# Decoder trunk: the second half of the output projection computed as the first half is, two column chunks at a time with seven products for two of its row pairs

## The chip, the cores and the metric

The kernel runs on one core of a Trainium2 chip. The metric is the device time of one execution in microseconds (us). One execution was recorded by the hardware profiler; all rows shown are from that one.

## The reference

Two layers work on x (256 tokens x 2048, float32). Each layer computes

```
h   = RMSNorm(x)
P   = h @ W_in                 2048 x 6144: [q | k | v | gate_B | gate_C | conv_in]
A   = differential attention (8 heads, relative bias)
Cv  = gate_B * causal_conv3(gate_C * conv_in)
x   = x + concat([A, Cv]) @ W_out             2048 x 2048
x   = x + (relu(RMSNorm(x) @ W_up) ** 2) @ W_down     2048 x 8192, 8192 x 2048
```

The change touches `x + concat([A, Cv]) @ W_out` alone, and the moment at which the norm after it is prepared.

## The kernel before

Every float32 operand is split into a high and a low part in the format that TensorE multiplies (ACT copies the high part, DVE subtracts it from the value), and each product is made of three matmuls, high x high, high x low, low x high (`TERMS`). A matmul has 128 rows of the contraction, 128 tokens and 512 columns. Tokens come in two blocks of 128 (`t`), x in four column chunks of 512 (`xs[0]` to `xs[3]`).

*The output projection.* The contraction over 2048 rows goes in eight pairs of 128-row blocks. Chunks 0 and 1 are computed side by side by `BySeven.project` (L824), chunks 2 and 3 one after the other by `linear` (L390 to L409, called at L986). `project` holds two accumulators of two PSUM banks each, one for each chunk. Six row pairs are ordinary: 24 matmuls for two chunks (`plain`, L830). The other two (pairs 4 and 5, the first two of the convolution's four) are computed as a 2 x 2 block product with seven products in place of eight (`seven`, L852): sums of the blocks of activations are made beforehand (`sums_of`), sums of the blocks of weights in the jobs of L778, and four of the seven products go to banks of their own (three from the pool `ps`, tag `bank`, one with tag `av`); the other three go straight into the accumulators. After the last seven, `e1` to `e4` are made from these four banks by ACT and DVE (L892 to L896) and added to x (L895 and L902).

*The order.* `self.order` (L756 to L760) lists the steps: pairs 0 and 1 for chunk 0, then for chunk 1; seven, pair, seven, pair; then the last two pairs for chunk 0 and for chunk 1. When chunk 0 is complete (`done`), its accumulators and the e-terms are added to x. PE runs its instructions in the order in which the program records them; a scheduler orders ACT, DVE and the DMA queues.

*Weights.* `Weights.take` (L374) makes the splits of weights three steps ahead (`AHEAD`). Each plain step loads 512 KB into one of four `raw` buffers, by SP's queue, and a load waits until the split of the load four before it has read its buffer. The split halves stand in three buffers each (`hi`, `lo`). A seven takes two raw buffers at once and keeps them until its sums are made; it makes three splits of 1024 columns and one of 512.

*The norm after it.* `Norm.chunk` (L465) prepares one chunk of x for the up projection: squares on ACT, then eight 128x128 transposes on PE into two banks of the pool `ps` (tag `bank`, three banks in all, shared with the sevens' products), and four splits of 128x256 on each of ACT and DVE (`split_gained`, L287 and L288). `work.start(piece, wait)` puts it into a background list that counts ticks; a plain step has two ticks. At the end of `project`, chunk 0 is asked for after 2 ticks and chunk 1 after 4, both with 2 more of their own; chunks 2 and 3 are asked for when each is complete. After the last chunk, `Norm.factors` sums the squares (DVE), takes the power on POOL, and copies the result on DVE.

*The up projection* begins right behind (L1159). Its column 0 runs over rows of chunks 0 and 1 first, for two column blocks, then over chunks 2 and 3. Its weights come in 1 MB loads into four buffers; two of them lie where the projection's temporary tiles lay.

Of the kernel before, what the change touches and what calls it, by code (L numbers as in the profile page):

```python
# [9 lines left out]
F32 = mybir.dt.float32  # L10
# [5 lines left out]
P = 128  # L16
DEPTH = 2
D = 2048
S = 256
NT = S // P  # L20
# [8 lines left out]
CH = 512  # L29
# [93 lines left out]
def trunk(ctx: ExitStack, tc: tile.TileContext, x, w_in, w_out, conv_w, q_norm_g, k_norm_g,  # L123
# [19 lines left out]
    def bank(name):  # L143
        return ps.tile([P, CH], F32, tag="bank", name=name)
# [600 lines left out]
    class BySeven:  # L745
# [3 lines left out]
        def __init__(self, l, bpool, weights):  # L749
            self.l, self.pool, self.weights = l, bpool, weights  # L750
            n = D // (4 * P)
            seven = [n + q for q in GATED]
            plain = [i for i in range(2 * n) if i not in seven]


            self.order = [(n, i) for n in range(2) for i in plain[:2]]  # L756
            self.order += [step for i, j in zip(plain[2:], seven)
                           for step in (("seven", j), ("pair", i))]
            self.order += [("pair", i) for i in plain[2 + len(seven):-2]]
            self.order += [(n, i) for n in range(2) for i in plain[-2:]]  # L760
            self.sums = []

        def sums_of(self, q, y):
# [11 lines left out]
            nc.scalar.activation(hi, v, AF.Copy)  # L775
            nc.vector.tensor_sub(lo, v, hi.bitcast(F32))

        def jobs(self, w, i):  # L778

            mine = {}  # L780

            def split(hi, lo, src):
                nc.scalar.activation(hi, src, AF.Copy)
                nc.vector.tensor_sub(lo, src, hi.bitcast(F32))
                return hi, lo

            def two(pool, tag, name, src):

                room = pool.tile([P, 2, 2, CH], F32R, tag=tag, name=name)
                hi, lo = split(room[:, 0], room[:, 1], src)  # L790
                return [(hi[:, j], lo[:, j]) for j in range(2)]

            def plain():
                raws = []
                for n in range(2):
                    raw = self.weights.pool.tile([P, 2, CH], F32, tag="raw", name="raw", bufs=RAW)
                    nc.sync.dma_start(
                        raw, w[2 * P * i:2 * P * (i + 1), n * CH:(n + 1) * CH].rearrange(
                            "(k p) c -> p k c", p=P))
                    raws.append(raw)  # L800
                mine["raw"] = raws
                b11, b21 = two(self.pool, "b", "w7b", raws[0])
                hi = wpool.tile([P, 2, CH], F32R, tag="hi", name="whi")
                lo = wpool.tile([P, 2, CH], F32R, tag="lo", name="wlo")
                return b11, b21, split(hi[:, 0], lo[:, 0], raws[1][:, 1])

            def sums():
                left, right = mine["raw"]
                t = mine["t"] = self.pool.tile([P, 4, CH], F32, tag="b", name="w7t")

                nc.vector.tensor_sub(t[:, 0], right[:, 0], left[:, 0])
                nc.vector.tensor_sub(t[:, 1], right[:, 1], right[:, 0])
                made = two(apool, "a", "w7x", t[:, 0:2])

                nc.vector.tensor_add(t[:, 2], t[:, 1], left[:, 0])
                nc.vector.tensor_sub(t[:, 3], left[:, 1], t[:, 2])
                return made

            def more():
                return two(apool, "a", "w7y", mine["t"][:, 2:4])  # L820

            return [plain, sums, more]

        def project(self, cat, norm, kpool, tmp):  # L824
            weights = self.weights
            both = [mm.tile([P, NT, CH], F32, tag="mm2", name=f"o{self.l}{n}") for n in range(2)]
            accs = [[acc[:, t] for t in range(NT)] for acc in both]
            prods = {2: accs[0][0], 4: accs[0][1], 3: accs[1][0]}

            def plain(i, n):  # L830
                hi, lo = weights.take()
                for j in range(2):
                    k = 2 * i + j
                    a = cat[k // KG]
                    while not a.ready:
                        work.tick()
                    for t in range(NT):
                        for m, (pa, pw) in enumerate(TERMS):
                            nc.tensor.matmul(  # L839
                                accs[n][t], a.ap[:, pa, k % KG, t * P:(t + 1) * P],  # L840
                                (hi, lo)[pw][:, j], start=(k == 0 and m == 0),
                                stop=(i == last and j == 1 and m == 2))
                    work.tick()
# [8 lines left out]
            def seven(i, start, end):  # L852
                if start:
                    for n in (1, 5, 6):
                        prods[n] = bank(f"po{self.l}{n}")
                    prods[7] = ps.tile([P, CH], F32, tag="av", name=f"po{self.l}7", bufs=1)
                b11, b21, b22 = weights.take()
                t1, t3 = weights.take()
                t2, t4 = weights.take()
                for n, a, b in ((1, A11, b11), (2, A12, b21), (3, S4, b22), (5, S1, t1),  # L860
                                (7, S3, t3), (6, S2, t2), (4, A22, t4)):
                    own = n in (1, 5, 6, 7)
                    for m, (pa, pw) in enumerate(TERMS):
                        nc.tensor.matmul(prods[n], form(i, pa, a), b[pw],
                                         start=(start and own and m == 0),
                                         stop=(end and own and m == 2))
                    if n == 5:
                        work.tick()
                work.tick()

            def onto(n):
                for t in range(NT):
                    nc.vector.tensor_add(xs[n][:, t], accs[n][t], xs[n][:, t])

            last = self.order[-1][1]
            steps = [i for what, i in self.order if what == "seven"]
            done = [j for j, (what, i) in enumerate(self.order) if what == 0][-1]
            for j, (what, i) in enumerate(self.order):
                if what == "pair":
                    plain(i, 0)  # L880
                    plain(i, 1)
                elif what == "seven":
                    seven(i, i == steps[0], i == steps[-1])
                    if i == steps[-1]:

                        x11, x21, x12, x22 = (xs[n][:, t] for n in range(2) for t in range(NT))


                        room = tmp.tile([P, 2, CH], F32, tag="ao", name="es", bufs=1)
                        e1, e2, e3 = room[:, 0], wide("e2"), room[:, 1]  # L890
                        e4 = kpool.tile([P, CH], F32, tag="kL", name="es4")
                        nc.scalar.activation(e1, prods[1], AF.Copy)  # L892
                        nc.vector.tensor_add(e2, prods[6], e1)
                        nc.vector.tensor_add(e4, prods[5], e2)
                        nc.vector.tensor_add(x22, prods[5], x22)  # L895
                        nc.vector.tensor_add(e3, prods[7], e2)  # L896
                else:
                    plain(i, what)
                    if j == done:
                        onto(0)  # L900
                        for x_, e in ((x11, e1), (x12, e4), (x21, e3), (x22, e3)):
                            nc.vector.tensor_add(x_, x_, e)  # L902
            onto(1)
            for n in range(2):
                work.start(norm.chunk(n, 2), 2 * n + 2)


    def mixer(l, norm, loads):

        with ExitStack() as scope:  # L910
# [15 lines left out]
            for q in range(AW // WC):  # L926
                weights.turned(w_in[l], 3 * AW + q * WC)
            by_seven = BySeven(l, bpool, weights)
            for what, i in by_seven.order:
                if what == "seven":  # L930
                    weights.jobs += by_seven.jobs(w_out[l], i)
                    continue
                for n in ((0, 1) if what == "pair" else (what,)):
                    weights.plain(w_out[l], 2 * P * i, n * CH, 2)
            for n in range(2, D // CH):
                weights.straight(w_out[l], 0, D // P, n * CH)
            loads(weights)

            bias = biasp.tile([P, 2 * NH, S], F32, tag="bias", name="bias")
# [41 lines left out]
                    by_seven.sums_of(q, ys[:, q])  # L981

            mnorm = Norm(1, l)
            by_seven.project(cat, mnorm, kpool, tmp)
            for n in range(2, D // CH):
                acc = linear(f"o{l}{n}", cat, weights)  # L986
                for t in range(NT):
                    nc.vector.tensor_add(xs[n][:, t], acc[:, t], xs[n][:, t])
                work.start(mnorm.chunk(n, 2))
        return mnorm  # L990

    def mlp(l, mnorm, last):
# [479 lines left out]
```

## Time and profile before

| what | us |
|---|---|
| time, median of three runs (2124.51 to 2621.47) | 2124.92 |
| the profiled execution's own time | 2124.95 |
| its span, first to last instruction | 2123.2 |
| PE busy | 2117.0 |
| DVE busy | 1724.5 |
| ACT busy | 1377.2 |
| POOL busy | 159.2 |
| output projection of layer 0, chunks 0 and 1 (from, to) | 298.3, 340.5 |
| output projection of layer 0, chunks 2 and 3 (from, to) | 340.5, 386.9 |
| output projection of layer 1, first matmul | 1353.8 |

PE is TensorE, PEld its weight loads, which overlap with it, DVE VectorE, ACT ScalarE, POOL GpSimd, SP the queue that issues most DMAs. Matmuls are pipelined: one lasts 0.39 us, and the next starts 0.23 us after it. So busy time of PE does not count matmuls; their starts do. In rows of the timeline stand the start, the duration, engine, line, operation, what it writes and reads, and the count of merged instructions; in brackets the idle time before it and who ended it. In rows of groups stand busy time and the mean in ns of one.

### The profile page before, as it was taken

How to read it: one execution, taken by the hardware profiler on the slowest of the kernel's cores; microseconds unless marked ns; L12 is line 12 of the kernel's file. 1: busy time of each engine (PE TensorE's matmuls, PEld its weight loads, DVE VectorE, ACT ScalarE, POOL GpSimd, SP SyncE). 2: the span in 40 equal slices, each digit the busy share in tenths (PEclk: the TensorE clock that was granted, in tenths of full speed). 3: DMA queues.
4: the chain of work that ended last, by engine and by line, in shares of the span. 5: the costliest groups of instructions: out<-in, count | busy, mean ns of one | idle time of the engine just before them, and what ended most of it. 6: DMA issues, size and time to landing. Idle time of an engine off the chain costs nothing.

```text
span 2123.2 us, 29201 instructions
## 1 busy us (share of the span) xinstructions
PE 2117.0 (100%) x10857; PEld 1809.9 (85%) x10857; DVE 1724.5 (81%) x2388; ACT 1377.2 (65%) x1828; POOL 159.2 (7%) x226
## 2 busy tenths in 40 slices
PE   9999999999999999999999999999999999999999
PEld 7888888888888888888888888888888888888887
DVE  6777676798888888799766776767988888888997
ACT  6767555677777776666566765556677677675664
POOL 3010100000000000011101101000000000000110
PEclk9999999999999999999999999999999999999999
DMA  8556667677777777788656565666877777777993
GB/s 272 179 167 191 196 191 229 214 252 224 231 233 231 236 230 231 250 301 290 217 170 182 165 208 179 197 209 221 260 233 232 232 230 232 233 230 259 319 310 104
DMA packets 297743, 476.01 MB, mean 224 GB/s; under 512 B 12707, under 2 KB 193781, under 8 KB 297600
## 3 DMA queue, kind: packets, MB, share of 16 engines
q1 hardware_dynamic: 269120, 406.76, 60.7%
q0 software_dynamic: 28288, 67.24, 10.0%
q8 instruction: 85, 1.39, 0.3%
q14 instruction: 58, 0.48, 0.1%
q10 hardware_dynamic: 192, 0.15, 0.0%
HBM read 440.52 MB, written 33.58 MB: 223 GB/s over the span
## 4 chain that ended last, share of the span: by engine, by line
PE 99%; DMA 0%; DVE 0%; SPq 0%; ACT 0%; issue 0%; DVEq 0%
PE upc L1159 31%; PE pr L1202 14%; PE dn L1283 8%; PE ci L430 4%; PE gc L430 4%; PE gb L430 4%; PE k L405 4%; PE v L405 4%; PE o L405 4%; PE q L405 4%; PE o L839 3%; PE dn L1365 2%; PE dn L1202 2%; PE pr1r L1202 2%; PE pr0r L1202 1%; PE up L1159 1%
## 5 line engine op out<-in xcount | busy, mean ns | idle before, releaser
L320 DVE TENSOR_TENSOR wlo<-raw,whi 128x1024 fp32r<-128x1024 f32 x266 | 322.1, 1222 | 188.3 <-ACT whi L319 118.3
L1159 PE MATMUL upc<-nT,uhi 128*128 128x512 f32 x1920 | 454.7, 389 | 0.0
L319 ACT ACTIVATE whi<-raw 128x1024 fp32r<-128x1024 f32 x266 | 281.5, 1059 | 240.6 <-PE gb L430 28.2
L1159 PEld LDWEIGHTS upc<-nT,uhi 128*128 128x128 f32 x1920 | 360.3, 188 | 74.7
L1023 DVE TENSOR_TENSOR ulo<-uraw,uhi 128x1024 fp32r<-128x1024 f32 x256 | 311.8, 1221 | 119.3 <-ACT f L1191 89.4
L1022 ACT ACTIVATE uhi<-uraw 128x1024 fp32r<-128x1024 f32 x256 | 270.6, 1057 | 159.7 <-PE upc L1159 138.1
L1159 PEld LDWEIGHTS upc<-nT,ulo 128*128 128x128 f32 x1920 | 246.2, 191 | 9.4
L1159 PE MATMUL upc<-nT,ulo 128*128 128x256 f32 x1920 | 249.1, 283 | 0.0
L1283 PE MATMUL dn<-whi,fb 128*128 128x512 f32 x496 | 156.7, 389 | 0.0
L1048 ACT ACTIVATE b2h<-draw 128x1024 fp32r<-128x1024 f32 x83 | 88.2, 1062 | 48.5 <-PE pr L1202 41.3
L319 ACT ACTIVATE whi<-uraw 128x1024 fp32r<-128x1024 f32 x62 | 65.9, 1063 | 81.8 <-PE dn L1283 66.0
L1283 PEld LDWEIGHTS dn<-whi,fb 128*128 128x128 f32 x496 | 93.1, 188 | 19.3
L1169 ACT ACTIVATE ev<-upc 128x512 f32<-128x512 f32 x120 | 72.0, 600 | 54.0 <-PE upc L1159 54.0
L1048 ACT ACTIVATE t24h<-t 128x1024 fp32r<-128x1024 f32 x83 | 88.3, 1063 | 22.8 <-PE pr L1202 15.9
L1049 DVE TENSOR_TENSOR t24l<-t,t24h 128x1024 fp32r<-128x1024 f32 x83 | 101.1, 1218 | 1.7
L1049 DVE TENSOR_TENSOR b2l<-draw,b2h 128x1024 fp32r<-128x1024 f32 x83 | 100.9, 1215 | 1.1 <-ACT b2h L1048 1.1
L1049 DVE TENSOR_TENSOR t13l<-t,t13h 128x1024 fp32r<-128x1024 f32 x83 | 101.0, 1217 | 0.7
L1062 DVE TENSOR_TENSOR t<-draw 128x1024 f32<-128x1024 f32 x83 | 101.1, 1218 | 0.3
L1048 ACT ACTIVATE t13h<-t 128x1024 fp32r<-128x1024 f32 x83 | 88.4, 1065 | 13.3 <-DVE t L1062 2.9
L1283 PE MATMUL dn<-wlo,fb 128*128 128x512 f32 x248 | 96.5, 389 | 0.0
L1202 PE MATMUL pr<-t13h,f 128*128 128x512 f32 x240 | 93.8, 391 | 0.0
L320 DVE TENSOR_TENSOR wlo<-uraw,whi 128x1024 fp32r<-128x1024 f32 x62 | 75.7, 1222 | 18.0 <-ACT whi L319 17.6
(452 smaller groups left out, 4292.8 us busy)
## 6 DMA issues: line engine op xcount, KB each, us to landing
uraw<-in_w_up_dram SPq DMA_DIRECT2D x128, 1024.0 KB, 6.2
raw<-in_w_in_dram SPq DMA_DIRECT2D x191, 512.0 KB, 4.0
draw<-in_w_down_dram SPq DMA_DIRECT2D x174, 512.0 KB, 5.3
raw<-in_w_out_dram SPq DMA_DIRECT2D x64, 512.0 KB, 4.4
uraw<-in_w_down_dram SPq DMA_DIRECT2D x62, 512.0 KB, 5.7
raw<-in_w_down_dram SPq DMA_DIRECT2D x10, 1024.0 KB, 5.5
hid0p<-f POOLq DMA_DIRECT2D x19, 512.0 KB, 3.6
fb<-hid0p POOLq DMA_DIRECT2D x19, 512.0 KB, 6.8
```

The lines of the kernel that those rows point to most:

```text
L319: pair = (nc.scalar.activation(hi, raw, AF.Copy), nc.vector.tensor_sub(lo, raw, hi.bitcast(F32)))
L320: nc.vector.tensor_sub(lo, raw, hi.bitcast(F32)))
L405: nc.tensor.matmul(acc[:, t], a.ap[:, pa, k % KG, t * P:(t + 1) * P], (hi, lo)[pw][:, j], start=(k == 0 and (pa, pw) == (0, 0)), stop=(k = ...
L430: nc.tensor.matmul(acc[:, f, 0] if part else acc[:, f], wt[:, k % 4, fs], a.ap[:, 0, k % KG] if part else a.ap[:, :, k % KG], start=(part ...
L1022: pair = (nc.scalar.activation(hi, src, AF.Copy), nc.vector.tensor_sub(lo, src, hi.bitcast(F32)))
L1023: nc.vector.tensor_sub(lo, src, hi.bitcast(F32)))
L1048: keep(nc.scalar.activation(hi, src, AF.Copy))
L1049: keep(nc.vector.tensor_sub(lo, src, hi.bitcast(F32)))
L1062: keep(nc.vector.tensor_sub(t[:, 0:2], raw[:, :, 1], raw[:, 0]))
L1159: nc.tensor.matmul(acc[:, 0] if part else acc, wt[part][:, k], a.ap[:, 0, k % KG] if part else a.ap[:, :, k % KG], start=(part == 0 and kh ...
L1202: nc.tensor.matmul(prods[n], f[:, pa, a], b[pw], start=(start and m == 0), stop=(stop and m == 2))
L1283: nc.tensor.matmul(prods[p], f[:, pa, 2 * k + t], b[pw][:, n], start=(p in starts and k == 0 and m == 0), stop=(stop and k == 1 and m == 2))
```

## The change

`BySeven` keeps one order for each half of the columns. Half 0 has the order of before. Half 1 (chunks 2 and 3) has the same steps with each seven behind an ordinary pair. `project` is called for both halves and takes the half's number `g`; `linear` is not used for w_out any more. The chunks 0 and 1 of the norm are asked for after 2 and 6 ticks (2 and 4 before). Chunk 2 is asked for when it is complete, two plain steps before chunk 3 is, chunk 3 at the end as before. The additions of the e-terms to x have the order x11, x21, x12, x22 (x11, x12, x21, x22 before).

```
-            self.order = [(n, i) for n in range(2) for i in plain[:2]]
-            self.order += [step for i, j in zip(plain[2:], seven)
-                           for step in (("seven", j), ("pair", i))]
-            self.order += [("pair", i) for i in plain[2 + len(seven):-2]]
-            self.order += [(n, i) for n in range(2) for i in plain[-2:]]
+            self.orders = []
+            for g in range(2):
+                chunks = (2 * g, 2 * g + 1)
+                order = [(n, i) for n in chunks for i in plain[:2]]
+                for i, j in zip(plain[2:], seven):
+                    order += [("seven", j), ("pair", i)][::-1 if g else 1]
+                order += [("pair", i) for i in plain[2 + len(seven):-2]]
+                order += [(n, i) for n in chunks for i in plain[-2:]]
+                self.orders.append(order)
...
-        def jobs(self, w, i):
+        def jobs(self, w, i, col):
...
-                        raw, w[2 * P * i:2 * P * (i + 1), n * CH:(n + 1) * CH].rearrange(
+                        raw, w[2 * P * i:2 * P * (i + 1),
+                               col + n * CH:col + (n + 1) * CH].rearrange(
...
-        def project(self, cat, norm, kpool, tmp):
+        def project(self, g, cat, norm, kpool, tmp):
...
-                    plain(i, what)
+                    plain(i, what - 2 * g)
                     if j == done:
                         onto(0)
-                        for x_, e in ((x11, e1), (x12, e4), (x21, e3), (x22, e3)):
+                        for x_, e in ((x11, e1), (x21, e3), (x12, e4), (x22, e3)):
                             nc.vector.tensor_add(x_, x_, e)
+                        if g:
+                            work.start(norm.chunk(2 * g, 2), 2)
             onto(1)
+            if g:
+                work.start(norm.chunk(2 * g + 1, 2))
+                return
             for n in range(2):
-                work.start(norm.chunk(n, 2), 2 * n + 2)
+                work.start(norm.chunk(n, 2), 4 * n + 2)
...
-            for what, i in by_seven.order:
-                if what == "seven":
-                    weights.jobs += by_seven.jobs(w_out[l], i)
-                    continue
-                for n in ((0, 1) if what == "pair" else (what,)):
-                    weights.plain(w_out[l], 2 * P * i, n * CH, 2)
-            for n in range(2, D // CH):
-                weights.straight(w_out[l], 0, D // P, n * CH)
+            for g, order in enumerate(by_seven.orders):
+                for what, i in order:
+                    if what == "seven":
+                        weights.jobs += by_seven.jobs(w_out[l], i, 2 * g * CH)
+                        continue
+                    for n in ((2 * g, 2 * g + 1) if what == "pair" else (what,)):
+                        weights.plain(w_out[l], 2 * P * i, n * CH, 2)
...
-            by_seven.project(cat, mnorm, kpool, tmp)
-            for n in range(2, D // CH):
-                acc = linear(f"o{l}{n}", cat, weights)
-                for t in range(NT):
-                    nc.vector.tensor_add(xs[n][:, t], acc[:, t], xs[n][:, t])
-                work.start(mnorm.chunk(n, 2))
+            for g in range(2):
+                by_seven.project(g, cat, mnorm, kpool, tmp)
```

In the changed program the instructions of both layers stand in the same order on PE, ACT and DVE, and outside of the two output projections and the first column of the up projection the order on every engine is that of before. The order around the two places of which the prediction speaks, with what an instruction waits for:

```
PE: 2 steps of chunk 2; 8 transposes of x[0]; 2 steps of chunk 3; 4 transposes of x[1];
    4 transposes of x[1]  [wait: DVE's split of k = 1 of x[0], the last reader of the first bank]
ACT: squares of x[1]; whi; w7b [wait: its raw load]; whi; nT_0 k0, k2; whi; nT_0 k1, k3; ...
DVE: wlo; wlo; w7b; wlo; nT_0 k0; w7t, w7t; nT_0 k2; wlo; nT_0 k1; w7t; nT_0 k3; ...

PE: last product of chunk 3; 8 transposes of x[2]; 8 matmuls up; 4 transposes of x[3];
    4 transposes of x[3]  [wait: DVE's split of k = 1 of x[2]]; 8 matmuls up; ...
ACT: uhi; nT_2 k0; squares x[3]; nT_2 k2; squares x[3]; uhi; nT_2 k1; ...
DVE: x[3] +=; x[3] +=; ulo; nT_2 k0, k2; tot; rowf [wait: POOL]; nT_2 k1; ...
```

More of the change, by code (lines that the diff above doesn't have):

```diff
@@ L822, in jobs @@
             return [plain, sums, more]
-        def project(self, cat, norm, kpool, tmp):
-            weights = self.weights
-            both = [mm.tile([P, NT, CH], F32, tag="mm2", name=f"o{self.l}{n}") for n in range(2)]
+        def project(self, g, cat, norm, kpool, tmp):
+            weights, order = self.weights, self.orders[g]
+            both = [mm.tile([P, NT, CH], F32, tag="mm2", name=f"o{self.l}{2 * g + n}")
+                    for n in range(2)]
             accs = [[acc[:, t] for t in range(NT)] for acc in both]
@@ L854, in seven @@
                     for n in (1, 5, 6):
-                        prods[n] = bank(f"po{self.l}{n}")
-                    prods[7] = ps.tile([P, CH], F32, tag="av", name=f"po{self.l}7", bufs=1)
+                        prods[n] = bank(f"po{self.l}{g}{n}")
+                    prods[7] = ps.tile([P, CH], F32, tag="av", name=f"po{self.l}{g}7", bufs=1)
                 b11, b21, b22 = weights.take()
@@ L872, in onto @@
                 for t in range(NT):
[L873 to L878, printed above, removed]
+                    nc.vector.tensor_add(xs[2 * g + n][:, t], accs[n][t], xs[2 * g + n][:, t])
+            last = order[-1][1]
+            steps = [i for what, i in order if what == "seven"]
+            done = [j for j, (what, i) in enumerate(order) if what == 2 * g][-1]
+            for j, (what, i) in enumerate(order):
                 if what == "pair":
@@ L884, in project @@
                     if i == steps[-1]:
-                        x11, x21, x12, x22 = (xs[n][:, t] for n in range(2) for t in range(NT))
+                        x11, x21, x12, x22 = (xs[2 * g + n][:, t]
+                                              for n in range(2) for t in range(NT))
                         room = tmp.tile([P, 2, CH], F32, tag="ao", name="es", bufs=1)
```

## The prediction

> **What bounds the kernel now.** I read the page first, then who waited for whom on PE, then the chain, then the busy time by stage, and last the rows of the stages that change.
>
> ```profile
> span 2123.2 us, 29201 instructions
> PE 2117.0 (100%) x10857; PEld 1809.9 (85%) x10857; DVE 1724.5 (81%) x2388; ACT 1377.2 (65%) x1828; POOL 159.2 (7%) x226
> PE 99%; DMA 0%; DVE 0%; SPq 0%; ACT 0%; issue 0%; DVEq 0%
> L320 DVE TENSOR_TENSOR wlo<-raw,whi 128x1024 fp32r<-128x1024 f32 x266 | 322.1, 1222 | 188.3 <-ACT whi L319 118.3
> L319 ACT ACTIVATE whi<-raw 128x1024 fp32r<-128x1024 f32 x266 | 281.5, 1059 | 240.6 <-PE gb L430 28.2
> raw<-in_w_out_dram SPq DMA_DIRECT2D x64, 512.0 KB, 4.4
> ```
> ```profile
> PE warm L177 <- DVE mhalf L169: 1.1, 1, 1.1
> PE tpb L505 <- DMA x<-in_x_dram: 0.5, 1, 0.5
> PE q L405 <- DVE wlo L320: 0.3, 1, 0.3
> PE q L405 <- DVE wlo L346: 0.2, 1, 0.2
> ```
> ```profile
> 324.37 16.32 PE o L839 x72
> ```
> ```profile
> 298.00:340.50 42.50, 42.50 (x191) 35.26 (x190) 36.28 (x42) 21.81 (x26) 0.00 (x0) 1.00 0.68 217
> 340.50:387.00 46.50, 46.50 (x218) 38.62 (x217) 26.98 (x32) 24.20 (x36) 0.00 (x0) 1.00 0.49 154
> ```
>
> TensorE sets the end: 99% of the chain is PE, and its four waits add up to 2.1 us, all at the start of the kernel. So time is products times their pace, plus any new wait of PE. The pace is 16.32/72 = 0.227 us for one 128x512 product. The two windows are the halves of the output projection of layer 0 (columns PE, PEld, DVE, ACT, POOL): the first has the sevens already, with DVE busy 36.28 of 42.50 us, and PE never waits there; the second, which changes, has DVE at 26.98 of 46.50.
>
> **The products (a gain).** A pair of rows costs two column chunks x 2 row blocks x 2 token blocks x 3 terms = 24 products, a seven 7 x 3 = 21. Two sevens per layer, two layers: 12 products fewer, 12 x 0.227 = 2.7 us, 1.36 us per layer, all on the path. Transposes and additions onto x keep their number.
>
> **The extra work beside it (nothing by its sum).**
>
> ```profile
> 303.11 0.69 DVE L812 TENSOR_TENSOR w7t<-raw 128x512 f32<-128x512 f32 x1
> 307.79 0.68 DVE L784 TENSOR_TENSOR wlo<-raw,whi 128x512 fp32r<-128x512 f32 x1
> ```
>
> A seven needs three splits of 1.22, one of 0.68 and four sums of 0.69 us on DVE, 7.1 us, in place of two splits, 2.4: 9.4 us more for two. The e-terms add eight operations of 0.69, 5.5 us. DVE comes to 26.98 + 14.9 = 41.9 of 46.5 - 1.36 = 45.1 us. ACT gains 2 x (1.06 x 1.5) + 0.6 = 3.8, 28.0 us. So on average both hide under PE, with 3 us to spare on DVE. If that cover were gone, each us over 45.1 would be a us of PE. What decides is the order inside.
>
> **Wait A: the transposes of chunk 1.** The pool of single PSUM banks has three. In the changed order chunk 0's transposes come after the two steps of chunk 2, as now; chunk 1's come later, after the two steps of chunk 3; and between them DVE and ACT make the first seven's weights. Chunk 0 takes two banks, chunk 1's first four transposes the third, and its last four wait until DVE has read chunk 0's first bank to the end (the last split of that bank). Everything behind them on PE's queue waits too.
>
> ```profile
> 340.52 0.39 PE L405 MATMUL o<-whi,cat 128*128 128x512 f32 x1
> 345.97 1.03 PE L476 MATMUL tpn<-ident,x 128*128 128x128 f32 x8
> 346.76 0.48 PE L405 MATMUL o<-whi,cat 128*128 128x512 f32 x1
> ```
> ```profile
> 341.93 1.21 DVE L320 TENSOR_TENSOR wlo<-raw,whi 128x1024 fp32r<-128x1024 f32 x1
> 348.45 0.87 DVE L288 SCALAR_TENSOR_TENSOR nT<-tpn,gains,nT 128x256 fp32r<-128x256 f32 x2
> ```
> ```profile
> 343.17 0.37 SPq L360 DMA_DIRECT2D raw<-in_w_out_dram  x1
> ```
> ```profile
> 299.21 1.06 ACT L783 ACTIVATE w7b<-raw 128x1024 fp32r<-128x1024 f32 x1 [1.48 <-DMA raw<-in_w_out_dram]
> ```
>
> When PE gets there: 340.52, two steps of 12 products (2.72 each), 0.79 for eight transposes (345.97 to 346.76), two steps, 0.40 for four: 352.6. When DVE gets there: the seven needs two raw buffers of the four. Its first load waits for the split at 341.93, and is issued where the trace issues a load now, at 343.17; with the median 4.4 us it lands at 347.57. On ACT's queue the split of this load (w7b) stands ahead of the next plain split and of chunk 0's four splits, so ACT sits idle for the load, as the row at 299.21 shows it doing for 1.48 us in the first half. w7b ends on ACT at 348.6. Then DVE has, in this order (durations less about 0.08, by which the next operation starts before one ends): w7b 1.14, a plain split 1.14, a chunk 0 split 0.40, two sums 0.60 each, a chunk 0 split 0.40, a plain split 1.14, and the split that frees the bank, 0.48: 5.9 us, until 354.6. PE waits 354.6 - 352.6 = **2.0 us**. Both sides:
>
> ```profile
> raw<-in_w_out_dram SPq DMA_DIRECT2D x1, 512.0 KB, 3.7
> ```
> ```profile
> raw<-in_w_out_dram SPq DMA_DIRECT2D x1, 512.0 KB, 7.3
> ```
>
> The first is a load issued alone at the end of this stage, the second one issued 1.4 us behind a 1 MB load of w_up. That big load moves away, so I take the median: 1.3 us with 3.7, 4.9 with 7.3. The first seven then starts 2 us late with its weights ready: PE reaches its third group of fresh banks at 363.8, chunk 1's last split ends about 361.8. No second wait there.
>
> **Wait B: the transposes of chunk 3.** Now chunk 2's transposes run early in the linear of chunk 3, some 20 us before its end. In the changed order chunk 2 is finished only 24 products before chunk 3. Its transposes take two banks right after the last product, eight products of the up projection follow, and chunk 3's transposes come then: the first four take the third bank, the last four wait until DVE has read chunk 2's first bank.
>
> ```profile
> 386.64 0.39 PE L405 MATMUL o<-whi,cat 128*128 128x512 f32 x1
> 386.87 1.98 PE L1159 MATMUL up<-nT,uhi 128*128 128x512 f32 x8
> 388.69 1.03 PE L476 MATMUL tpn<-ident,x 128*128 128x128 f32 x8
> ```
> ```profile
> 387.07 1.06 ACT L1022 ACTIVATE uhi<-uraw 128x1024 fp32r<-128x1024 f32 x1 [1.66 <-PE o L405]
> 388.04 0.61 ACT L494 ACTIVATE junk<-x 128x512 f32<-128x512 f32 x1
> 388.65 0.61 ACT L494 ACTIVATE junk<-x 128x512 f32<-128x512 f32 x1
> 390.21 0.81 ACT L287 ACTIVATE nT<-tpn,gains 128x256 fp32r<-128x256 f32 x2
> ```
> ```profile
> 387.07 1.29 DVE L988 TENSOR_TENSOR x<-o,x 128x512 f32<-128x512 f32 x2 [0.40 <-PE o L405]
> 388.28 1.21 DVE L1023 TENSOR_TENSOR ulo<-uraw,uhi 128x1024 fp32r<-128x1024 f32 x1
> 389.41 0.15 DVE L517 TENSOR_REDUCE tot<-ss 128x2 f32<-128x8 f32 x1
> ```
> ```profile
> 389.65 0.19 POOL L450 TENSOR_SCALAR row_e<-tot 128x2 f32<-128x2 f32 x1 [127.11 <-DVE tot L517]
> 389.92 0.69 POOL L452 TENSOR_TENSOR row_r<-row_e,mhalf 128x2 f32<-128x2 f32 x1
> ```
>
> In the clock of these rows PE is ready for the last four at 388.69 + 0.79 + 0.40 = 389.9. ACT's queue from 387.07: uhi 0.97, chunk 2 split 0.40, squares of x 0.61, chunk 2 split 0.40, squares 0.61, uhi 0.97, and the split of the second half of the first bank from 391.0 to 391.5. DVE's queue: the additions, ulo until 389.4, two chunk 2 splits until 390.3, the sum over squares at about 390.2, then a copy that waits for POOL's two operations (in the rows, 389.41 to 390.61: 1.2 us), so until 391.5. Both queues meet there; the freeing split runs 391.55 to 392.05. PE waits 392.05 - 389.9 = **2.2 us**. From below: without the copy ahead of it ACT's 391.5 alone keeps the wait at about 2.1. From above: POOL 0.3 later, 2.5.
>
> **The loads that move on SP's queue (nothing).** Two 1 MB loads of w_up, issued among the loads of w_out now, move behind all loads of w_out. The first waits for the addition of e4 after the last seven, about 8.5 us before the last product ends (387.03 in this clock), the second for the addition of e3 to chunk 2, about 1.7 before. Behind them on SP stand the next w_up load and six of w_down, which wait for the last product anyway.
>
> ```profile
> uraw<-in_w_up_dram SPq DMA_DIRECT2D x4, 1024.0 KB, 7.5
> ```
> ```profile
> 395.35 1.06 ACT L1022 ACTIVATE uhi<-uraw 128x1024 fp32r<-128x1024 f32 x1 [0.91 <-PE up L1159]
> 398.42 1.06 ACT L1022 ACTIVATE uhi<-uraw 128x1024 fp32r<-128x1024 f32 x1 [2.02 <-PE up L1159]
> ```
>
> With 7.5 us the second lands 5.8 after the last product; ACT wants it 11.4 after (398.42), and 3 us later still behind wait B. The cover is over 5 us; a load twice as long would eat it, 2 us per layer. The second pair of accumulators is free when chunk 0 and 1 are added to x, 4 us before their first product.
>
> **Sum.** Per layer -1.36 + 2.0 + 2.2 = +2.8. The two layers have the same order on every engine, so +5.7 us. The profiled execution took 2124.95 us for its span of 2123.2 (1.75 around it); it stands 0.03 above the median 2124.92. 2124.95 + 5.7 = 2130.6.
>
> **Rivals.**
> 1. *The gain stays* (faster than before): PE reaches both places after DVE. Wait A is gone if the load takes 2.4 us, B if the chain on ACT is 2.2 us shorter. For it: the first half hides the same sevens, and PE waits nowhere in it. Against it: no load row is under 3.7, and the first half has no norm transposes in its order. 2124.95 - 2.7 = 2122.2; with one of the waits gone 2126.2 to 2126.6.
> 2. *The clock drops after a wait.* PE slows down when it has sat idle, and each of four waits costs more than its length. Against it: the granted clock is 1.00 in both windows (the last column but two). But the longest wait of PE listed is 1.1 us. A length for such a stretch can only be borrowed, from the warm-up at the kernel's start:
>
> ```profile
> 1.05 3.78 PE L177 MATMUL warm<-ones 128*128 128x128 f32 x16 [1.05 <-DVE mhalf L169]
> ```
>
> That is 0.236 us for a matmul of 128 columns, against 0.79/8 = 0.099 for a transpose of the same size, 2.4 times. If 3.8 us after each wait ran so, 2.2 more each, 8.8: 2139.4. [...]
> 3. *The first seven's load is late.* With 7.3 us wait A is 4.9: 2 x 2.9 more, 2136.4. It is the 1 MB load ahead that made that row, and it has moved, so little speaks for it.
> 4. *DVE becomes the bound of the stage* (slower by over 2%): 42.5 us would be needed, 21 per layer, that is 66 us of DVE in a stage of 45; the count above gives 41.9.
>
> **How the numbers follow.** Forecast (both waits, no more) 0.62, its own range 2129.0 to 2132.6, from A of 1.3 (load of 3.7) to 2.7 (as far the other way) and B of 2.1 to 2.5. Rival 1 0.20, half of it with one wait left; rival 2 0.07; rival 3 0.08; rest, rival 4 in it, 0.03. The range 2121.8 to 2135.0 takes in rival 1 and leaves out rivals 2 and 3 and the rest, 0.18. Changes under 2% (42 us) are about what a measurement of this kernel does not tell from no change: within 2% 0.97, faster 0.01, slower 0.02.
>
> **What would show it.** PE 10845 products; the waits of PE list the transposes of L476 behind the DVE split L288, four times, near 2 us each, two of them near 352 and 389; ACT's w7b idle for a raw load near 347; a seven at 0.227 per product; the two w_up loads after the last w_out load; granted clock 1.00. It is wrong if PE's waits stay at 2.1 us (rival 1), if products after a wait take over 0.227 (rival 2), or if PE waits at another place, at a seven's bank or an up split.

## The result and the profile after

The changed kernel takes 2131.37 us (median, 2129.62 to 2132.88), the kernel before 2124.84 in the same comparison: ratio 1.0031, 95% interval 1.0022 to 1.0040. It is slower, by 6.5 us (0.3%), and the forecast was 2130.6. The interval is about 0.1% either way, so a change well under the 2% of the prediction can be told from none. One of the eight executions of before took 2621.47 us, far from the other seven (2124.51 to 2124.92), and nothing here explains it. The profiled execution of after took 2130.75 us; its ledger below is against the profiled one of before (2124.95).

From the page of after: span, busy time, and the chain that ended last.

```profile
span 2129.0 us, 29231 instructions
PE 2116.8 (99%) x10845; PEld 1809.3 (85%) x10845; DVE 1750.0 (82%) x2428; ACT 1384.6 (65%) x1838; POOL 159.6 (7%) x226
PE 97%; DVE 1%; DMA 1%; issue 0%; ACT 0%; SPq 0%; POOL 0%; DVEq 0%; POOLq 0%
```

Twelve matmuls fewer (10857 before), as counted. PE's share of the chain falls from 99% to 97%: DVE and DMA stand in it now, so PE waits in the middle of the kernel. Who waits for whom on PE in after (us in total, times, longest):

```profile
PE tpn L476 <- DVE ratio L527: 3.9, 2, 2.0
PE tpn L476 <- DVE nT L288: 2.7, 2, 1.7
PE warm L177 <- DVE mhalf L169: 1.1, 1, 1.1
```

Four new waits, all of the transposes of the norm. The waits put down to `ratio` are for a split too: `ratio` is a row of 0.16 us on DVE that the transposes do not read, and it starts 0.47 us after the split L288 that frees the bank. The transposes start 0.15 us after the end of that split, as at the other place (0.14). The timeline of PE in after, layer 0:

```profile
345.79 1.04 PE L476 MATMUL tpn<-ident,x 128*128 128x128 f32 x8
...
352.14 0.60 PE L476 MATMUL tpn<-ident,x 128*128 128x128 f32 x4
353.72 0.63 PE L476 MATMUL tpn<-ident,x 128*128 128x128 f32 x4 [0.98 <-DVE nT L288]
...
388.22 0.60 PE L476 MATMUL tpn<-ident,x 128*128 128x128 f32 x4
390.78 0.63 PE L476 MATMUL tpn<-ident,x 128*128 128x128 f32 x4 [1.96 <-DVE ratio L527]
391.17 1.77 PE L1166 MATMUL up<-nT,ulo 128*128 128x256 f32 x8
392.73 3.03 PE L1166 MATMUL up<-nT,uhi 128*128 128x512 f32 x8
```

and in layer 1:

```profile
1410.83 0.60 PE L476 MATMUL tpn<-ident,x 128*128 128x128 f32 x4
1413.11 0.63 PE L476 MATMUL tpn<-ident,x 128*128 128x128 f32 x4 [1.69 <-DVE nT L288]
...
1447.61 0.60 PE L476 MATMUL tpn<-ident,x 128*128 128x128 f32 x4
1450.18 0.63 PE L476 MATMUL tpn<-ident,x 128*128 128x128 f32 x4 [1.96 <-DVE ratio L527]
1450.56 1.19 PE L1166 MATMUL up<-nT,ulo 128*128 128x256 f32 x8
1451.59 2.00 PE L1166 MATMUL up<-nT,uhi 128*128 128x512 f32 x8
```

The cost of a wait is the distance of the two starts less the 0.40 that four transposes take: wait A 1.18 and 1.88 us, wait B 2.16 and 2.17. One thing more differs between the layers: behind wait B the same eight `uhi` matmuls last 3.03 in layer 0 and 2.00 in layer 1. The busy time by microsecond there (columns PE, PEld, DVE, ACT, POOL, then the granted clock) says why:

```profile
388.00:391.00 3.00, 1.04 (x8) 0.74 (x7) 1.91 (x9) 2.82 (x7) 0.89 (x2) 1.00 1.00 314
391.00:392.00 1.00, 1.00 (x9) 1.00 (x8) 0.96 (x5) 0.81 (x2) 0.00 (x0) 0.75 1.00 317
392.00:393.00 1.00, 1.00 (x6) 1.00 (x5) 0.75 (x3) 0.28 (x2) 0.00 (x0) 0.50 1.07 407
393.00:394.00 1.00, 1.00 (x3) 0.73 (x3) 1.00 (x1) 0.23 (x1) 0.00 (x0) 0.50 1.01 410
394.00:395.00 1.00, 1.00 (x4) 0.79 (x3) 0.59 (x2) 0.00 (x0) 0.00 (x0) 0.54 1.05 410
395.00:396.00 1.00, 1.00 (x8) 0.86 (x7) 0.00 (x0) 0.15 (x1) 0.00 (x0) 1.00 1.02 401
```

The granted clock is 0.50 from about 391.5 to 394.9, 3.4 us. From the start of the first `ulo` group to that of the eighth group of up matmuls it takes 11.19 us (391.17 to 402.36), in layer 1 9.63 (1450.56 to 1460.19): the drop costs 1.56. The ledger: -2.72 for the products, 3.06 for the waits A, 4.33 for the waits B, 1.56 for the one drop: +6.2, against 5.8 between the profiled times.

A drop lowers a run's mean clock by 0.5 x 3.4/2129 = 0.0008, so the mean clock counts the drops of each run: 1.000 none, 0.999 one, 0.998 two. With three digits that is a rough count: one of the 67 runs of before beside the experiments reads 0.999 too, at an ordinary 2125.25 us. Of eight runs of after, two had none (2129.62, 2129.69), four one (2130.75 to 2132.3), two two (2132.76, 2132.88). The median holds about one.

### The profile page after: what moved, and what is told of

It is laid out like the page before. It is cut to its first block, busy times and chain, and to the rows that moved or that the text cites. A ratio compares the mean times of both kernels' runs of the same rounds, so it can differ in the third digit from the quotient of the medians.

```text
span 2129.0 us, 29231 instructions
## 1 busy us (share of the span) xinstructions
PE 2116.8 (99%) x10845; PEld 1809.3 (85%) x10845; DVE 1750.0 (82%) x2428; ACT 1384.6 (65%) x1838; POOL 159.6 (7%) x226
## 4 chain that ended last, share of the span: by engine, by line
PE 97%; DVE 1%; DMA 1%; issue 0%; ACT 0%; SPq 0%; POOL 0%; DVEq 0%; POOLq 0%
PE upc L1166 31%; PE pr L1209 14%; PE dn L1290 8%; PE o L845 5%; PE ci L430 4%; PE gc L430 4%; PE gb L430 4%; PE k L405 4%; PE v L405 4%; PE q L405 4%; PE dn L1372 2%; PE dn L1209 2%; PE pr1r L1209 2%; PE pr0r L1209 1%; PE upw L1166 1%; PE pr L1290 1%
## 5 line engine op out<-in xcount | busy, mean ns | idle before, releaser
L320 DVE TENSOR_TENSOR wlo<-raw,whi 128x1024 fp32r<-128x1024 f32 x258 | 312.3, 1223 | 165.6 <-ACT whi L319 95.6
L319 ACT ACTIVATE whi<-raw 128x1024 fp32r<-128x1024 f32 x258 | 273.2, 1060 | 230.5 <-PE o L845 35.9
L845 PE MATMUL o<-whi,cat 128*128 128x512 f32 x384 | 121.0, 390 | 0.0
```

Source lines behind the costliest of these rows:

```text
L319: pair = (nc.scalar.activation(hi, raw, AF.Copy), nc.vector.tensor_sub(lo, raw, hi.bitcast(F32)))
L320: nc.vector.tensor_sub(lo, raw, hi.bitcast(F32)))
L845: nc.tensor.matmul(accs[n][t], a.ap[:, pa, k % KG, t * P:(t + 1) * P], (hi, lo)[pw][:, j], start=(k == 0 and m == 0), stop=(i == last and ...
```

## Experiments

Theory: the change saves its products, 2.7 us, and loses 7.4 us to two waits per layer, both for a PSUM bank that the transposes need and that a late split still reads; a drop of the clock behind a wait adds 1.6 us each time. Rivals: the sevens' extra work on DVE and ACT delays PE at other places too; PE stalls for the splits whatever bank they read; the order of the steps and not the bank makes the loss. All ratios below are against the kernel before, measured beside each. Where an edit stands ahead of the transposes, lines are higher by three or more (L479 for L476).

**1. Wait B alone taken away** (b_bank). The last four transposes of chunk 3 write the bank of tag `av`, which no one uses there, in place of the third bank of the pool.

```
+                if self.which and (n, j) == (3, 1):
+                    tp = ps.tile([P, CH], F32, tag="av", name=f"tpn{n}_{j}", bufs=1)
+                else:
                     tp = bank(f"tpn{n}_{j}")
```

> The changed kernel with one edit: the last four transposes of chunk 3 write to the bank with tag av, which nobody uses at that time, so that they need not wait for chunk 2's first bank. Theory (bank waits): wait B (2.17 us per layer) is gone, wait A stays (1.2 and 1.9 us in the two layers). 2124.9 - 2.7 + 3.1 = 2125.3 us. If the clock falls only after waits of about 2 us, the granted clock is 1.000 in all runs. Rival (the clock falls after any wait of over 1 us): 2125.3 plus 1.6 for each drop, up to 2128.5, with clocks of 0.999. Rival (the load on DVE and ACT is the cause, not the bank): the wait only moves to chunk 3's splits, near the eighth product of the second half of column 0, and the time stays near 2129.6.

2125.40 us (2124.72 to 2126.11), ratio 1.0001, interval 0.9992 to 1.0010. The mean clock was 1.000 in all eleven runs. In b_bank's list of PE's waits only wait A is left of the four, 1.40 and 1.69 us:

```profile
PE tpn L479 <- DVE nT L288: 3.1, 2, 1.7
```

So a free bank takes wait B away entirely, though the split itself is no earlier. With wait B went the drops as well, 6.0 us in all: 4.3 of waiting and 1.6 of clock.

**2. Wait A alone taken away** (a_bank): the same edit with `(1, 1)` for `(3, 1)`, chunk 1's last four transposes.

> The changed kernel with one edit: the last four transposes of chunk 1 write to the bank with tag av, free until the sevens' fourth product. Theory (bank waits): wait A is gone, wait B stays at 2.17 us per layer. 2124.9 - 2.7 + 4.3 = 2126.5 us, plus 1.6 for each of 0 to 2 drops of the clock: 2126.5 to 2129.7, with clocks from 1.000 to 0.998. Rival (load on DVE and ACT): the wait goes to the first seven, whose weights or fourth bank come late, and the time stays at 2129.6 or over.

2128.70 us (2126.67 to 2130.18), ratio 1.0017 (1.0008 to 1.0026). The two waits left are B's:

```profile
PE tpn L479 <- DVE ratio L530: 3.9, 2, 2.0
```

Of eleven runs two had no drop (2126.67 and 2127.06, where 2126.5 was expected), five had one, four had two: 13 drops behind 22 waits of 1.97 us. Behind the 22 waits of 1.4 and 1.7 us in b_bank there was none. The lengths are from one profile of each kernel.

**3. Both taken away** (ab_bank): the edit in `((1, 1), (3, 1))`.

> Both edits at once. Theory (bank waits): no wait of PE is left in the second half, the products saved show whole: 2124.9 - 2.7 = 2122.2 us, clock 1.000 in all runs; faster than both kernels. Rival (load on DVE and ACT, 40.1 of 47.5 us busy in the half): new waits of 0.5 us or more per layer at the sevens or at chunk 3's splits, 2123.5 or over. Rival (the clock drops are not made by waits): clocks under 1.000 remain.

2122.71 us (2121.86 to 2123.52), ratio 0.9988 (0.9980 to 0.9997), the clock 1.000 throughout. This is the gain of the products, and the kernel beats both. What is left of PE's waits is a new one: the fourth product of the first seven wants the `av` bank that chunk 1 now uses.

```profile
PE po L873 <- DVE nT L288: 0.7, 2, 0.4
```

**4. The bank taken elsewhere** (c_bank): `((0, 1), (3, 1))`. Chunk 0's second four transposes write `av`, so chunk 1 finds two banks free, and `av` is free again sooner.

> As ab_bank (2122.7), but in the norm of the second half it is chunk 0's second bank, not chunk 1's, that is written under the tag av (and chunk 3's second bank as before). Theory of the banks: chunk 1's four transposes then have a free bank of the three, and av is free again some 3 us sooner for the fourth product of the first seven, so the 0.42 and 0.32 us that ab_bank still waited there go: no wait over 0.3 us in either layer's second half, clock 1.000, 2122.0. Rival (the splits on VectorE are late whatever bank they read): the wait moves to the sevens' first products, which then need chunk 0's and chunk 1's banks of the three: 2122.7 or more.

2121.96 us (2121.63 to 2122.49), ratio 0.9986 (0.9978 to 0.9995). The longest waits of PE in c_bank are those of the kernel's start, as in before; none of the norm or of a seven is listed:

```profile
PE warm L177 <- DVE mhalf L169: 1.1, 1, 1.1
PE q L405 <- DVE wlo L320: 0.3, 1, 0.3
```

2.96 us below before, where the products account for 2.72. So neither the extra work on DVE and ACT nor the loads that moved cost anything measurable.

**5. The change without its sevens** (no_seven): after's order, chunks side by side, but in the second half the two sevens are ordinary pairs.

```
-                for i, j in zip(plain[2:], seven):
-                    order += [("seven", j), ("pair", i)][::-1 if g else 1]
+                if g:
+                    order += [("pair", i) for i in (2, 4, 3, 5)]
+                else:
+                    for i, j in zip(plain[2:], seven):
+                        order += [("seven", j), ("pair", i)]
...
```

> The changed kernel with the second half's order kept side by side, but its two sevens computed as ordinary pairs. Theory: wait A is made by the seven's first weights in ACT's and DVE's queues, so it is gone; wait B belongs to the side-by-side order and stays at 2.0 to 2.2 us per layer; no products are saved: 2124.9 + 4.3 = 2129.2 us, plus 1.6 for each of 0 to 2 drops of the clock. Rival (the sevens make both waits): 2124.9, no wait.

2130.66 us (2128.76 to 2132.54), ratio 1.0026 (1.0016 to 1.0036). Wait A is gone: the eight transposes of chunk 1 run in one piece. Wait B stands.

```profile
352.57 1.03 PE L476 MATMUL tpn<-ident,x 128*128 128x128 f32 x8
...
391.38 0.63 PE L476 MATMUL tpn<-ident,x 128*128 128x128 f32 x4 [1.97 <-DVE ratio L527]
```

So wait A belongs to the sevens' weights, wait B to the side-by-side order alone. In this place the sevens earn 2.7 us and pay 3.1 by wait A: after is no faster with them than without them.

**6. The chunks asked for as before** (ask4): "asked for later" undone.

```
-                work.start(norm.chunk(n, 2), 4 * n + 2)
+                work.start(norm.chunk(n, 2), 2 * n + 2)
```

> The change with one part undone: the second half's norm chunks are asked for as early as before (2n + 2 ticks instead of 4n + 2), so chunk 1's eight transposes stand some 12 products (2.7 us) earlier in TensorE's queue. Theory: the split that frees their bank hangs on the chain of weight loads on ScalarE and VectorE (it ends at about 353.6 in the profile after) and not on TensorE, so TensorE only arrives earlier and waits longer: wait A of 3.7 to 4.4 us instead of 1.2 to 1.9, that is 2129.6 + 2 x 2.7 = 2135, and up to 4 clock drops at 1.6 each, 2135 to 2141. Rival (the splits are taken in the order of the chunks, so that an earlier chunk is split earlier and the wait stays as it is): 2131.4, as after.

2140.56 us (2136.9 to 2143.16), ratio 1.0072 (1.0059 to 1.0084). Wait A in ask4, on PE:

```profile
346.40 1.03 PE L476 MATMUL tpn<-ident,x 128*128 128x128 f32 x8
...
350.03 0.60 PE L476 MATMUL tpn<-ident,x 128*128 128x128 f32 x4
354.43 1.08 PE L476 MATMUL tpn<-ident,x 128*128 128x128 f32 x4 [3.80 <-DVE nT L288]
...
1418.41 1.09 PE L476 MATMUL tpn<-ident,x 128*128 128x128 f32 x4 [3.91 <-DVE nT L288]
```

Counted from chunk 0's transposes (346.40 here, 345.79 in after) chunk 1's first four come 3.63 us on instead of 6.35, 2.7 sooner, and the bank comes when it came, 8.03 on instead of 7.93. So the split that frees it does not hang on TensorE's place in the order but on the chain of weights, and the wait is longer by what PE is sooner. The profiled run is the slowest of its five (2143.16 us). In it the clock is low from 352.7 to 359.6, 6.8 us, and as long in layer 1 (stretches of the profile of ask4; the clock is the last column but two, and 0.78 over 3.8 us is 1.7 us of 0.50):

```profile
350.60:354.40 3.80, 0.03 (x1) 0.01 (x1) 3.80 (x8) 2.85 (x5) 0.00 (x0) 0.78 0.46 140
354.40:360.00 5.60, 5.57 (x16) 4.59 (x17) 5.26 (x9) 2.26 (x4) 0.00 (x0) 0.54 0.58 161
...
1414.50:1418.40 3.90, 0.00 (x1) 0.02 (x1) 3.90 (x8) 2.92 (x5) 0.00 (x0) 0.91 0.41 134
1418.40:1425.00 6.60, 6.59 (x19) 5.35 (x20) 5.39 (x9) 2.55 (x5) 0.00 (x0) 0.54 0.53 161
```

So asking later is worth 9.2 us to the change: 5.0 of waiting (7.7 us of idle in the waits A here, 2.7 in after), the rest by the clock.

**7. The same with a free bank** (c_ask4): c_bank with ask4's line.

> c_bank (2121.96) with the chunks asked for as early as in ask4. Theory: with av taken by chunk 0 no transpose waits for a bank, so it makes no difference when they are asked for: 2121.6 to 2122.5, no wait of 0.4 us or more on TensorE in either half, clock 1.000. Rival (the earlier splits push the seven's weight splits back on VectorE): waits at the first seven's products of 1 us or more, 2124 and up.

2121.81 us (2121.58 to 2122.19), ratio 0.9986 (0.9977 to 0.9995). With the bank there, it makes no difference when the chunks are asked for: the moment mattered because of the bank. c_bank and c_ask4 are the fastest versions; with ab_bank they are the three that beat both kernels.

**8. The seven ahead of its pair** (seven_first): in the second half the order of the first.

```
-                    order += [("seven", j), ("pair", i)][::-1 if g else 1]
+                    order += [("seven", j), ("pair", i)]
```

> The change with each seven ahead of its pair in the second half too (as in the first half). The first seven then starts 5.3 us sooner, right behind chunk 1's transposes (354.35 instead of 359.66 in the profile after). Its first product needs the bank of chunk 0's last splits (read until 355.56 in the profile after), a later one that of chunk 1's (360.75 there, some 1.2 to 2.4 sooner if the pair's weight splits fall in behind). Theory: the pair ahead covers this chain; without it a wait of 1.2 to 4 us per layer at the seven's products, on top of waits A and B: 2134 to 2139, with clock drops at 1.6 each within. Rival: weights and banks are ready anyway, and the order is worth nothing: 2131.4.

2144.11 us (2142.56 to 2144.34), ratio 1.0089 (1.0075 to 1.0103): above what the theory and the rival gave. On PE the wait moved from the transposes to the seven's own banks; layer 0 in seven_first:

```profile
354.14 0.93 PE L870 MATMUL po<-w7b,cat 128*128 128x512 f32 x3 [0.59 <-DVE nT L288]
...
361.31 2.65 PE L870 MATMUL po<-w7x,sf 128*128 128x512 f32 x6 [4.86 <-DVE nT L288]
```

I had allowed 1.2 to 4 us per layer on top of wait A; it is 5.5 and 5.7 (0.65 and 5.07 in layer 1), without a wait A. What I missed is DVE's queue in seven_first: the sums and the first split for the second seven come ahead of chunk 1's splits.

```profile
355.22 0.69 DVE L816 TENSOR_TENSOR w7t<-raw 128x512 f32<-128x512 f32 x1 [1.22 <-DMA raw<-in_w_out_dram]
355.83 0.69 DVE L817 TENSOR_TENSOR w7t<-raw 128x512 f32<-128x512 f32 x1
356.43 1.22 DVE L788 TENSOR_TENSOR w7b<-raw,w7b 128x1024 fp32r<-128x1024 f32 x1
```

Idle time at these waits makes 8.5 of the 11.8 us between the profiled times (11.2 against 2.7 in after). The clock drops for 3.4 us at the long wait of layer 0 and for at least 6.0 at that of layer 1 (1424 to 1430), against 3.4 in all in after: at 1.56 us for each 3.4, that is 2.8 us more or over, most of the rest. The ordinary pair ahead of the seven saves 12.7 us: it is the cover under which the splits that free the banks are made.

**9 and 10. Longer waits B** (gap1 and gap3): a_bank with one or three unused copies of chunk 2's first bank on ACT ahead of the split on which wait B hangs, to see how the clock depends on the length (`range(3)` in gap3).

```
                 for i in range(2):
                     k = 2 * j + i
+                    if (self.which, n, j, i) == (1, 2, 0, 1):
+                        for c in range(1):
+                            nc.scalar.activation(wide(f"gap{c}")[:, :CH], tp, AF.Copy)
                     split_gained(...)
```

> a_bank (wait A gone, wait B of 1.97 us left; 2128.7) with one copy of chunk 2's first bank to a scratch tile on ScalarE ahead of the split that wait B hangs on: an unused copy, about 0.60 us (the row of the 128x512 evictions). Wait B becomes about 2.6 us in each layer, +1.2 in all without the clock. Theory (a wait of about 2 us lets the clock drop in part of the cases, a longer one in more): drops in at least as many of the waits as in a_bank (13 of 22), the median at 2126.7 + 1.2 + 1 to 2 drops at 1.6 = 2129.5 to 2131.1. Rival (the drop is not tied to the length of the wait): half of the waits drop as before, 2129.9; or a wait over 2.6 us always drops: 2131.1 in every run.

> As gap1 with three unused copies: wait B about 3.8 us in each layer, +3.6 in all without the clock (2130.3). Theory (longer waits drop the clock more surely): both waits drop in every run, 2130.3 + 2 x 1.6 = 2133.5 or more, the mean clock 0.998. Rival (length has no part in it): about half of the waits drop, runs spread over 2130.3, 2131.9 and 2133.5.

gap1: 2130.16 us (2128.3 to 2130.8), ratio 1.0023 (1.0014 to 1.0032); gap3: 2132.47 us (2130.29 to 2132.91), ratio 1.0034 (1.0021 to 1.0046). The waits grew by less than I had put, to 2.2 and 3.2 us (first row gap1, second gap3), 0.26 for the first copy and 0.5 for each other:

```profile
PE tpn L479 <- DVE nT L288: 4.5, 2, 2.2
```

```profile
PE tpn L479 <- DVE nT L288: 6.4, 2, 3.2
```

By the mean clocks, gap1 had two drops in six runs and one in five, 17 behind 22 waits; gap3 two in four runs and one in one, 9 behind 10. Behind the longer waits the share with a drop was larger in these counts (13 of 22 at 1.97 us in a_bank), and at 2.2 us 5 of 22 had none.

## Why the prediction was right

**The products.** 10845 matmuls, and c_bank, which keeps the change and loses its waits, stands 2.96 us under before. Predicted 2.7. Right.

**The extra work, hidden.** The second half in after (same columns as in the prediction):

```profile
340.50:388.00 47.50, 46.52 (x219) 38.56 (x218) 40.08 (x51) 28.28 (x42) 0.00 (x0) 1.00 0.55 165
```

DVE 40.08 of 47.50, predicted 41.9 of 45.1; ACT 28.28, predicted 28.0. (The window runs 2.5 us past the half's last product.) Over the whole kernel DVE gained 25.5 us (1750.0 against 1724.5), 12.8 per layer where the sum had 14.9: it added whole durations, though each of the 20 added operations starts about 0.08 before the last one ends, by the prediction's own reading, 1.6 us in all. PE waits nowhere in the window but at wait A. Right, and c_bank shows the cover holds when the waits are gone. No wait of ACT for a load of w_up is listed in after behind the two projections (380 to 460 us and 1440 to 1530): the loads that moved cost nothing, as put down.

**Wait A.** The mechanism is shown by a_bank (a free bank ends it) and no_seven (without sevens it does not arise). The size was one value for both layers, 2.0 from a load of 4.4 us. The loads that the seven's first split waits for, in after, layer 0 and then layer 1 (count, KB, us to landing):

```profile
raw<-in_w_out_dram SPq DMA_DIRECT2D x1, 512.0 KB, 3.6
```

```profile
raw<-in_w_out_dram SPq DMA_DIRECT2D x1, 512.0 KB, 4.3
```

```profile
346.60 1.06 ACT L787 ACTIVATE w7b<-raw 128x1024 fp32r<-128x1024 f32 x1 [2.22 <-DMA raw<-in_w_out_dram]
347.69 1.23 DVE L788 TENSOR_TENSOR w7b<-raw,w7b 128x1024 fp32r<-128x1024 f32 x1 [2.06 <-ACT w7b L787]
```

ACT and DVE sit idle for it as put down. Load 3.6, wait 1.18; load 4.3, wait 1.88: one for one, as the chain in the prediction has it (1.3 with 3.7, 2.0 with 4.4). The term was mis-sized by 0.8 us in layer 0, since the median load was taken where the bound with 3.7 held. Which layer has the shorter wait changes from run to run: in b_bank it is 1.69 us of idle in layer 0 and 1.40 in layer 1.

**Wait B.** Predicted 2.2, measured 2.16 and 2.17, with the bank as its cause by b_bank. The two queues meet as worked out; DVE in after:

```profile
390.08 0.17 DVE L520 COPY rowf<-row_r 128x2 f32<-128x2 f32 x1 [1.09 <-POOL row_r L452]
390.15 0.48 DVE L288 SCALAR_TENSOR_TENSOR nT<-tpn,gains,nT 128x256 fp32r<-128x256 f32 x1
```

**Rival 2, the clock.** The forecast had no drop, with 0.07 for four. The truth lies between: by the mean clocks 8 drops behind the 16 waits B of after's eight runs, and none behind the 22 waits A of 1.40 and 1.69 us in b_bank. By the prediction's own sign, products that take over 0.227 behind a wait, this rival is half right. The drop of after cost 1.56 us rather than the 2.2 borrowed from the warm-up; and the profile of before reads a granted clock of 1.00 over the warm-up (each stretch of 2 us from 0 to 12), so that row does not show a drop. This is the step of the prediction that failed: it took the clock to hold through waits of 2 us, which no run had shown (the longest wait of PE listed in before is 1.1 us), and behind the wait of 1.96 us in layer 0 of after the granted clock read 0.50.

**The sum.** The runs without a drop took 2129.6, 1.0 under the forecast, mostly wait A of layer 0 (0.8). About one drop in the median run gives the 1.6 back. So the mechanism of the two waits was right, but that the forecast came within 0.8 us was partly luck: two errors of opposite sign met. **Rival 1**, the gain stays, is what the change would have been with one more bank in each place: PE would reach both places before DVE still, and nothing would hang on it. **Rival 3** did not come: the two loads took 3.6 and 4.3. **Rival 4** did not come either, the time moved by 0.3%.

## What to carry to other kernels

When work of one stage is moved closer to its consumer, count the buffers between them, not only the busy time: here 13 us more of work per layer on DVE cost nothing, and a fourth PSUM bank in two places was worth 9 us. An ordinary step left ahead of a special one, or a request made later, can be what covers the chain that frees a buffer; take it away only with the buffer there (ask4 costs 9 us, c_ask4 nothing). In this kernel a wait of TensorE cost its length, and behind about half of the waits of 1.97 us (30 of 56) and 9 of 10 at 3.2 us the clock fell as well, which cost 1.56 us in after; behind the waits of 3.80 and 3.91 us in ask4 it was low twice as long, 6.8 us.

## What the runs showed of the hardware

The granted clock of TensorE read 0.50 behind waits much shorter than I had thought: in after from about 391.5 to 394.9, behind a wait of 1.96 us. Behind the wait of the same length in layer 1 of that profile it stayed at 1.00. Lengths from the profiles, drops by the mean clock of each run: waits of 1.4 to 1.7 us, 0 drops behind 22 (b_bank); 1.97 us, 13 behind 22 (a_bank; 30 behind 56 with the waits B of after and no_seven); 2.2 us, 17 behind 22 (gap1); 3.2 us, 9 behind 10 (gap3). These counts do not show what sets apart the waits with a drop: the shorter ones are all waits A and the longer ones all waits B.

Nor did a longer wait always bring a longer drop. Behind the waits B the clock was low for 3.4 us (layer 0 of after and of gap1, both layers of gap3 and ask4), behind 3.80 and 3.91 us in ask4 for 6.8, behind 4.86 us in layer 0 of seven_first for 3.4 again, and behind 5.07 us in its layer 1 for at least 6.0. Layer 0 of seven_first, where the wait ends at 361.31 (columns as above):

```profile
358.00:360.00 2.00, 0.00 (x0) 0.00 (x0) 2.00 (x4) 0.79 (x2) 0.00 (x0) 1.00 0.06 5
360.00:362.00 2.00, 0.69 (x2) 0.63 (x3) 2.00 (x5) 0.08 (x1) 0.00 (x0) 0.90 0.82 262
362.00:364.00 2.00, 2.00 (x6) 1.56 (x5) 0.15 (x1) 0.00 (x0) 0.00 (x0) 0.50 0.72 209
364.00:366.00 2.00, 2.00 (x8) 1.55 (x8) 0.85 (x1) 1.08 (x2) 0.00 (x0) 0.75 0.81 297
366.00:368.00 2.00, 2.00 (x11) 1.65 (x10) 1.30 (x2) 1.04 (x1) 0.00 (x0) 1.00 0.04 13
```

What decides whether the clock falls behind a wait, and for how long, no run here shows.
